# Layer 1 feed-forward: the up projection of 19 of its 22 tiles as seven block products

## The chip, the cores and the metric

The kernel runs on one core of a Trainium2 chip. The metric is the device time of one execution in microseconds; the median of three runs is given. The engines that matter are TensorE (matmuls, shown as PE, with its weight loads as PEld), VectorE (DVE), ScalarE (ACT), GpSimd (POOL) and the queue of DMA starts on SyncE (SP).

## The reference, cut to what matters

Two layers run over 640 token columns: 512 of a denoising sample and 128 of a prompt, side by side. Each layer is a mixer followed by a convolutional feed-forward. The change concerns the feed-forward of layer 1:

```python
def _conv_ffn(h, w_up, cw, cb, w_down):      # h: tokens x 1024, w_up: 1024 x 5632, w_down: 2816 x 1024
    a, g = jnp.split(h @ w_up, 2, axis=-1)   # a and g: tokens x 2816 each
    return (jax.nn.gelu(_dwconv3(a, cw, cb)) * g) @ w_down
...
h = _modulate(x, norm2_w[l], sh2, sc2)       # RMS norm, scale and shift
x = x + g2 * _conv_ffn(h, ...)
```

## The kernel before, in words

Everything is feature-major: a tile is 128 features (partitions) by 640 tokens (columns), and the columns are worked on as two halves of 320 (`HF`). The model width 1024 is 8 tiles (`KT`), the inner width 2816 is 22 tiles (`NF`).

Matmuls run on float32 split in two parts of type fp32r: hi is the rounded value, lo what is left of it. `wload` (L177) loads a weight tile of 128 x 1024, ScalarE casts it to hi (L181), and VectorE subtracts to get lo (L183); raw, hi and lo tiles have rings of three buffers each (`wraw`, `whi`, `wlo`). `proj` (L186, its matmul is L193) multiplies hi by hi, hi by lo and lo by hi, for each of the 8 k tiles and each half: 8 x 3 x 2 = 48 matmuls of 320 columns for one output tile of 640 columns.

`ffn` (L323) runs over the 22 tiles f. For each it makes two output tiles with `up` (L324), one of a and one of g: 96 matmuls. `hidden` (L333) copies a out of PSUM (L310), runs the three-tap convolution (ScalarE L313, four VectorE instructions L317 and L319, because the sample and the prompt are separate sequences), gelu (L336), the product with g (L337), and splits the result to hi and lo (L197, L198). The down projection goes by groups of 8, 7 and 7 tiles (`GROUPS`, L27). After the first tile of the next group, `down` (L342) makes all eight output tiles of the group before, and `residual` (L268, L273) adds each to x in three instructions (columns 0 to 320, 320 to 512, 512 to 640, since the gate of the prompt differs). The last group goes through `out_halves` (L276), which takes the halves one after the other, so that the norm of the first half can be made beside the matmuls of the second; it also squares the new x (L214) and sums on GpSimd (L215).

At its start `start_three` (L293) begins three up tiles on the first half while the norm of the second half is still being made (`norm_k`, L244).

PSUM has eight banks: three tiles of two banks for products (tag A twice, tag B once, L72) and two banks for all else (`misc`).

The order of instructions on each engine is fixed when the program is built: the tile framework takes instructions by priority (program order, moved by `tc.high_priority`) as their inputs and buffers become free in its own model of the engines. It can therefore put matmuls of a later step between those of an earlier one.

Of the kernel before, what the change touches and what calls it, by code (L numbers as in the profile page):

```python
# [8 lines left out]
F32 = mybir.dt.float32  # L9
# [36 lines left out]
def trunk(ctx: ExitStack, tc: tile.TileContext, I, O):  # L46
# [130 lines left out]
    def wload(src, n, key="w"):  # L177
        raw = wp.tile([P, 1024], F32, tag="wraw", name=nm("wraw"), bufs=3)
        nc.sync.dma_start(out=raw[:, :n], in_=src)
        hi = wp.tile([P, 1024], F32R, tag="whi", name=nm("whi"), bufs=3)  # L180
        S.copy(hi[:, :n], raw[:, :n])  # L181
        lo = wp.tile([P, 1024], F32R, tag="wlo", name=nm("wlo"), bufs=3)
        V.tensor_tensor(out=lo[:, :n], in0=raw[:, :n], in1=hi[:, :n], op=ALU.subtract)  # L183
        return hi, lo

    def proj(ps, hi, lo, hs, off=0, halves=(0, 1), ks=None):  # L186
        n = len(hs) if ks is None else KT
        for k in (range(n) if ks is None else ks):
# [54 lines left out]

    def norm_k(pool, xk, rb, l, js, jc, k, hl, a0, a1):  # L244
# [3 lines left out]
        hf = pool.tile([P, w], F32, tag="hf", name=nm("hf"), bufs=2)  # L248
# [5 lines left out]
        S.copy(hl[:, 0, a0:a1], hf)  # L254
        eng = G if k % 2 else V
        eng.tensor_tensor(out=hl[:, 1, a0:a1], in0=hf, in1=hl[:, 0, a0:a1], op=ALU.subtract)

# [18 lines left out]
    def out_halves(pool, x, src, n, l, j, ys, acc, xsrc, done):  # L276
        late = []
        for b in range(2):
            for o in range(KT):
                hi, lo = wload(src(o), n * P)  # L280
# [12 lines left out]
    def start_three(srcs, hs, late):  # L293
        tiles = []
        for i, src in enumerate(srcs):
            hi, lo = wload(src, KT * P)
# [11 lines left out]
    def conv3(pool, ps, w0, w1, w2, b, tag, bufs=2):  # L308
        a = pool.tile([P, NT], F32, tag=tag + "a", name=nm(tag + "a"), bufs=bufs)
        S.copy(h2(a), ps[:, :, :HF])  # L310
        t = pool.tile([P, NT], F32, tag=tag + "t", name=nm(tag + "t"), bufs=bufs)
# [10 lines left out]

    def ffn(pool, x, hs, l, acc, between, done, late):  # L323
        def up(f, s):  # L324
            for _ in range(1 + (f %3 == 1)):
                if between:
                    between.pop(0)()
            hi, lo = wload(I["w_up"][l, f, s], KT * P)
            ps = mm_tile()
            proj(ps, hi, lo, hs)  # L330
            return ps

        def hidden(f, pa, pg):  # L333
            w = [vc_("fcw", (l * 3 + i) * NF + f) for i in range(3)]
            _, t = conv3(pool, pa, w[0], w[1], w[2], vc_("fcb", l * NF + f), "fc")
            S.activation(out=t, in_=t, func=AF.Gelu_apprx_tanh)  # L336
            mark[0] = V.tensor_tensor(out=h2(t), in0=h2(t), in1=pg[:, :, :HF], op=ALU.mult)  # L337
            hl = hl_tile(hidp, "hid") if f % 10 < 9 else hl_tile(pool, "hidx", 1)
            hilo(hl, t)
            return hl  # L340

        def down(g, hid):  # L342
            f0, f1 = GROUPS[g]
            for o in range(KT):
                if between:
                    between.pop(0)()
                hi, lo = wload(I[f"w_down{g}"][l, o], (f1 - f0) * P)
                ps = mm_tile()
                proj(ps, hi, lo, hid)
                residual(x[o], ps, l, 5, o, 0, NT)  # L350

        first = start_three([I["w_up"][l, 0, 0], I["w_up"][l, 0, 1], I["w_up"][l, 1, 0]], hs, late)
        pend = None
        for g, (f0, f1) in enumerate(GROUPS):
            hid = []
            for f in range(f0, f1):
                pa = first.pop(0) if first else up(f, 0)
                pg = first.pop(0) if first else up(f, 1)
                hid.append(hidden(f, pa, pg))
                if pend is not None:  # L360
                    down(*pend)
                    pend = None
            pend = (g, hid)
        return out_halves(pool, x, lambda o: I["w_down2"][l, o], 7, l, 5, pend[1], acc, None, done)

    def mixer0(ctx0, pool, hs, ready):
# [18 lines left out]
        def token_major(name, evict, before=None):  # L385
            pss = [mm_tile() for _ in range(3)]
            for kk in range(KT // 2):
                if before is not None and kk == 0:
                    before(-1)
                hi, lo = wload(I[name][kk], 1024)  # L390
                for k2 in range(2):
# [47 lines left out]
        def gmlp(g):  # L439
            hi, lo = wload(I["w_gu"][g], KT * P)  # L440
            ps = mm_tile("B")
# [30 lines left out]
        def q_part(h):  # L472
            hi, lo = wload(I["w_qk"][0, h], KT * P)
            ps = mm_tile("B" if h else None)
            proj(ps, hi, lo, hs)
            raw = ap_.tile([P, NT], F32, tag="qraw", name=nm("qraw"), bufs=1)
            with tc.high_priority(300):
                S.activation(out=h2(raw), in_=ps[:, :, :HF], func=AF.Copy, scale=0.125)
            q = ap_.tile([P, NT], F32, tag="q", name=nm("q"), bufs=1)
            rope(q[:, :NS], raw[:, :NS])  # L480
            S.copy(q[:, NS:], raw[:, NS:])
            return q

# [120 lines left out]
    def mixer1(ctx1, gpool, hs, firsts):  # L604
# [98 lines left out]
        def head_in(h, hook=None):  # L703
            xcs, xch, xmh = [], [], []
            for i in range(2):
# [23 lines left out]
        def head_v(h, xmh):  # L729
            hi, lo = wload(I["w_hv"][h], 512)  # L730
            va = pool.tile([P, NCH, HD + 1], F32, tag="va", name=nm("va"), bufs=1)
# [14 lines left out]
        def head_qk(h, xch):  # L746
            hi, lo = wload(I["w_hqk"][h], 1024)
            qk = []
# [98 lines left out]
        def head_og(h, part=(0, 1)):  # L847
            sgs = []
            for o in (2 * h + i for i in part):
                hi, lo = wload(I["w_og"][o], KT * P)  # L850
                ps = mm_tile()
# [109 lines left out]
    with ExitStack() as c0:  # L961
# [17 lines left out]

        late = ffn(xp, x, hs, 0, acc, btw, done0, late)  # L980
        modx.close()
# [4 lines left out]
    with ExitStack() as c0:  # L986
        xp, x, acc = xpool(c0)
        hs = []
        late = out_halves(xp, x, lambda o: I["w_out1"][o], KT, 1, 2, ys, acc, xdr,
                   lambda b: norm_half(xp, x, acc, 1, 3, 4, hs, b))  # L990

        def done1(b):
# [7 lines left out]

            return rstd_steps(xp, acc, b, rb) + [lambda k=k: one(k) for k in range(KT)]

        for step in ffn(xp, x, hs, 1, acc, [], done1, late):
            step()
# [5 lines left out]
def _layout(i):  # L1010
# [67 lines left out]
    dn = np.asarray(i["w_down"])  # L1078
    for g, (f0, f1) in enumerate(GROUPS):
        a[f"w_down{g}"] = np.stack([wt(dn[l, f0 * P:f1 * P]) for l in range(2)])  # L1080
    t = np.arange(NS)
# [40 lines left out]
```

## Time and profile before

| | |
|---|---|
| median of three runs | 1606.1 us (1604.69 to 1607.99) |
| profiled execution, its own time | 1606.81 us |
| its span, first to last instruction | 1605.0 us |
| TensorE busy | 1561.2 us, 10560 matmuls |
| VectorE busy | 960.0 us |
| ScalarE busy | 712.7 us |
| GpSimd busy | 120.1 us |
| granted TensorE clock, mean | 0.992 |

Busy time is the union of an engine's instructions, so overlapping matmuls are not counted twice; a single matmul's duration is much longer than the distance at which matmuls follow one another. Layer 1's feed-forward runs from about 1100 us (its norm and its first up tiles) to the end. Idle time in brackets stands before an instruction, with the instruction that ended it.

### The profile page before, as it was taken

The page shows a single profiled execution, that of the slowest core. Times are in us where ns is not written, and L with a number is a line of the kernel's source. Part 1 is how long each engine was busy: PE and PEld are TensorE (multiplying, and loading weights), DVE is VectorE, ACT ScalarE, POOL GpSimd, SP SyncE. Part 2 cuts the span into 40 slices and gives each one's busy share as a digit, 9 for nine tenths or more (in the row PEclk, how much of TensorE's full clock was granted, in tenths as well). Part 3 has the DMA queues.
Part 4 walks back from the last instruction along what each step waited for, and adds up shares of the span by engine and source line. Part 5 has one row for each costly group of instructions (what it writes and reads, how often), then busy time and mean ns, then how long its engine had stood idle before and what let it go on. Part 6 is the DMA issues. An engine that isn't in the chain of part 4 may idle for free.

```text
span 1605.0 us, 26031 instructions
## 1 busy us (share of the span) xinstructions
PE 1561.2 (97%) x10560; PEld 1501.9 (94%) x10560; DVE 960.0 (60%) x1738; ACT 712.7 (44%) x1171; POOL 120.1 (7%) x116
## 2 busy tenths in 40 slices
PE   5999999999999999999989999999999999999997
PEld 4888889999999999999988999999999999999996
DVE  5547776769894889444775575667544334433445
ACT  5646665563312331334587564635633223312342
POOL 1100002300000000002300000013100000000012
PEclk9999999999999999999998999999999999999998
DMA  9424444436562555224523213234322222222233
GB/s 359 149 73 146 150 146 172 134 101 201 170 208 89 176 176 175 83 62 123 165 69 95 85 57 90 66 135 128 93 79 79 67 79 79 65 81 79 72 107 112
DMA packets 60167, 191.60 MB, mean 119 GB/s; under 512 B 6764, under 2 KB 10348, under 8 KB 59920
## 3 DMA queue, kind: packets, MB, share of 16 engines
q1 hardware_dynamic: 60048, 189.95, 37.2%
q8 instruction: 83, 1.36, 0.4%
q14 instruction: 36, 0.29, 0.1%
HBM read 181.95 MB, written 7.97 MB: 118 GB/s over the span
## 4 chain that ended last, share of the span: by engine, by line
PE 86%; DVE 6%; ACT 4%; issue 2%; DMA 2%; POOL 0%; SPq 0%; POOLq 0%; DVEq 0%; ACTq 0%
PE mm L193 72%; PE mm L827 2%; PE mm L805 2%; DVE wlo L183 1%; PE mm L401 1%; PE mm L403 1%; PE mm L802 1%; PE mm L402 1%; DMA mw<-w_mod 1%; PE misc L562 1%; ACT whi L181 1%; DVE xr L247 1%; ACT hf L252 1%; PE misc L109 1%; PE mm L532 1%
## 5 line engine op out<-in xcount | busy, mean ns | idle before, releaser
L193 PE MATMUL mm<-h,whi 128*128 128x320 f32 x3744 | 726.7, 312 | 3.4 <-ACT rows L612 1.6
L193 PEld LDWEIGHTS mm<-h,whi 128*128 128x128 f32 x3744 | 595.4, 189 | 9.7 <-ACT fca L310 1.9
L181 ACT CAST whi<-wraw 128x1024 fp32r<-128x1024 f32 (+2 forms) x229 | 233.0, 1019 | 586.6 <-PE mm L193 551.5
L193 PE MATMUL mm<-h,wlo 128*128 128x320 f32 x1872 | 444.8, 311 | 3.4 <-DVE wlo L183 3.4
L183 DVE TENSOR_TENSOR wlo<-wraw,whi 128x1024 fp32r<-128x1024 f32 (+2 forms) x229 | 272.7, 1191 | 232.8 <-ACT whi L181 226.3
L193 PE MATMUL mm<-hid,whi 128*128 128x320 f32 x1920 | 393.1, 310 | 1.8 <-ACT hid L197 0.7
L193 PEld LDWEIGHTS mm<-h,wlo 128*128 128x128 f32 x1872 | 318.9, 189 | 5.3 <-DVE wlo L183 4.2
L193 PEld LDWEIGHTS mm<-hid,whi 128*128 128x128 f32 x1920 | 310.4, 188 | 4.7 <-ACT hid L197 1.4
L193 PE MATMUL mm<-hid,wlo 128*128 128x320 f32 x960 | 255.5, 309 | 0.2 <-DVE wlo L183 0.2
L193 PEld LDWEIGHTS mm<-hid,wlo 128*128 128x128 f32 x960 | 169.7, 188 | 0.4 <-DVE wlo L183 0.4
L273 DVE SCALAR_TENSOR_TENSOR x<-mm,mod,x 128x192 f32<-128x192 f32 (+2 forms) x192 | 75.3, 433 | 139.9 <-PE mm L193 135.6
L136 DVE SCALAR_TENSOR_TENSOR mj<-mw,crow 128x1024 f32<-128x1024 f32 x112 | 136.6, 1219 | 1.0
L215 POOL TENSOR_TENSOR acc<-acc,sq 128x320 f32<-128x320 f32 x48 | 61.7, 1284 | 910.0 <-ACT sq L214 880.1
L337 DVE TENSOR_TENSOR fct<-fct,mm 128x640 f32<-128x640 f32 x44 | 36.1, 820 | 97.5 <-PE mm L193 94.1
L336 ACT ACTIVATE fct<-fct 128x640 f32<-128x640 f32 x44 | 32.3, 738 | 84.5 <-DVE fct L319 84.5
L252 ACT ACTIVATE hf<-xr,mod 128x192 f32<-128x192 f32 (+2 forms) x88 | 47.5, 575 | 22.6 <-DVE mod L174 8.8
L247 DVE TENSOR_TENSOR xr<-x,rb 128x320 f32<-128x320 f32 (+1 forms) x56 | 38.0, 694 | 24.9 <-ACT hf L252 13.7
L317 DVE SCALAR_TENSOR_TENSOR fct<-fca,vec,fct 128x511 f32<-128x511 f32 x88 | 44.9, 547 | 11.9 <-ACT fct L313 11.9
L319 DVE SCALAR_TENSOR_TENSOR fct<-fca,vec,fct 128x511 f32<-128x511 f32 x88 | 44.7, 544 | 0.0
L313 ACT ACTIVATE fct<-fca,vec 128x640 f32<-128x640 f32 x44 | 40.5, 925 | 1.3
L214 ACT ACTIVATE sq<-x 128x320 f32<-128x320 f32 x70 | 32.2, 468 | 16.7 <-DVE x L273 15.0
L541 ACT ACTIVATE p<-mm,mx 128x640 f32<-128x640 f32 (+1 forms) x40 | 28.4, 711 | 17.8 <-DVE mx L540 17.6
(249 smaller groups left out, 1491.6 us busy)
## 6 DMA issues: line engine op xcount, KB each, us to landing
wraw<-w_up SPq DMA_DIRECT2D x88, 512.0 KB, 3.7
mw<-w_modT SPq DMA_DIRECT2D x56, 512.0 KB, 4.3
wraw<-w_down SPq DMA_DIRECT2D x48, 448.0 KB, 3.3
mw<-w_mod SPq DMA_DIRECT2D x40, 512.0 KB, 5.9
wraw<-w_out SPq DMA_DIRECT2D x32, 512.0 KB, 3.6
wraw<-w_down SPq DMA_DIRECT2D x16, 512.0 KB, 3.6
x<-xT SPq DMA_DIRECT2D x16, 320.0 KB, 5.5
wraw<-w_qk SPq DMA_DIRECT2D x8, 512.0 KB, 3.5
```

The source lines that it names most:

```text
L136: V.scalar_tensor_tensor(out=junk, in0=w, scalar=1.0, in1=crow[:, r], op0=ALU.mult, op1=ALU.mult, accum_out=mod[:, l, j, k, r:r + 1])
L181: S.copy(hi[:, :n], raw[:, :n])
L183: V.tensor_tensor(out=lo[:, :n], in0=raw[:, :n], in1=hi[:, :n], op=ALU.subtract)
L193: T.matmul(ps[:, b, :HF], w, hs[k][:, part, b * HF:b * HF + HF], start=(k == 0 and i == 0), stop=(k == n - 1 and i == 2))
L215: (eng or V).tensor_tensor(out=acc[:, sl], in0=acc[:, sl], in1=sq, op=ALU.add)
L247: V.tensor_tensor(out=xr, in0=xk[:, a0:a1], in1=rb, op=ALU.mult)
L252: S.activation(out=hf[:, a:b], in_=xr[:, a:b], func=AF.Identity, scale=mod[:, l, jc, k, r:r + 1], bias=mod[:, l, js, k, r:r + 1])
L273: V.scalar_tensor_tensor(out=xo[:, a:b], in0=pa, scalar=mod[:, l, j, o, r:r + 1], in1=xo[:, a:b], op0=ALU.mult, op1=ALU.add)
L313: S.activation(out=t, in_=a, func=AF.Identity, scale=w1, bias=b)
L317: V.scalar_tensor_tensor(out=t[:, s + 1:e], in0=a[:, s:e - 1], scalar=w0, in1=t[:, s + 1:e], op0=ALU.mult, op1=ALU.add)
L319: V.scalar_tensor_tensor(out=t[:, s:e - 1], in0=a[:, s + 1:e], scalar=w2, in1=t[:, s:e - 1], op0=ALU.mult, op1=ALU.add)
L337: mark[0] = V.tensor_tensor(out=h2(t), in0=h2(t), in1=pg[:, :, :HF], op=ALU.mult)
```

## The change

Only layer 1's feed-forward is changed in its work; `wload` returns the raw tile too, layer 0 keeps its path. The first three tiles (`PLAIN`) are made as before. For the tiles 3 to 21 the two products a and g, each in two column halves, are seen as a 2 x 2 block product: the two rows are a and g, the inner index is the first and the second four k tiles, the columns are the two halves. They are made by seven block products of 4 k tiles x 3 passes = 12 matmuls of 320 columns, which need sums of weight blocks and sums of input blocks, and some of which are added to a bank that was read out before.

- Inputs: `fold_step`, four times, makes four combined input blocks (two subtractions, two combined instructions, two splits of 640 columns on VectorE, with two casts on ScalarE). They run among the three plain tiles.
- Weights: `weights(f)` loads four quarters of 256 KB, makes four sums of 512 columns on VectorE, and splits 1024 + 1024 + 1024 + 512 columns; the first two pairs use the rings `whi` and `wlo` that the down weights use as well. It is called one tile ahead.
- Banks: `fold_first`, `fold_main` and `fold_last` run the seven products into two banks of one PSUM tile and one `misc` bank. From f = 5 on that third bank begins with a ScalarE copy of the first product.
- Down: groups of 5, 5, 4, 4 and 4 tiles in layer 1; at most four (after a group of five) or three output tiles are made after each up tile. The last group, four tiles, goes through `out_halves`.
- The pool of layer 1's norm is closed after the plain tiles, and the fold's weight buffers take its place.

```diff
+GROUPS = (((0, 8), (8, 15), (15, 22)), ((0, 5), (5, 10), (10, 14), (14, 18), (18, 22)))
+PLAIN = 3
...
+        def prod(out, w, i, rhs, start):
+            for j in range(4):
+                c = slice(i * 512 + j * P, i * 512 + j * P + P)
+                for n, (h, part) in enumerate(((0, 0), (0, 1), (1, 0))):
+                    T.matmul(out, w[h][:, c], rhs(j, part), start=(start and j == 0 and n == 0),
+                             stop=(j == 3 and n == 2), skip_group_check=not start)
+
+        def split(w, src, n):
+            S.copy(w[0][:, :n], src[:, :n])
+            V.tensor_tensor(out=w[1][:, :n], in0=src[:, :n], in1=w[0][:, :n], op=ALU.subtract)
+            return w
+
+        def weights(f):
+            def pair(pool_, tag, n, bufs):
+                return [pool_.tile([P, n], F32R, tag=tag + p, name=nm(tag), bufs=bufs) for p in ("hi", "lo")]
+
+            ra, rb = (wp.tile([P, 1024], F32, tag="wraw", name=nm("wraw"), bufs=3) for _ in range(2))
+            rc = zp[0].tile([P, 1024], F32, tag="rc", name=nm("rc"), bufs=1)
+            rd = zp[0].tile([P, 512], F32, tag="rd", name=nm("rd"), bufs=2)
...
+            nc.sync.dma_start(out=rd, in_=src[1][:, hi_])
+            nc.sync.dma_start(out=ra[:, lo_], in_=src[0][:, lo_])
+            nc.sync.dma_start(out=rc[:, hi_], in_=src[1][:, lo_])
+            nc.sync.dma_start(out=rb[:, lo_], in_=src[0][:, hi_])
+            V.tensor_tensor(out=ra[:, hi_], in0=rc[:, hi_], in1=rd, op=ALU.add)
+            wa = split(pair(wp, "w", 1024, 3), ra, 1024)
+            V.tensor_tensor(out=rb[:, hi_], in0=ra[:, hi_], in1=ra[:, lo_], op=ALU.add)
+            wb = split(pair(wp, "w", 1024, 3), rb, 1024)
+            V.tensor_tensor(out=rc[:, hi_], in0=rc[:, hi_], in1=ra[:, lo_], op=ALU.add)
+            V.tensor_tensor(out=rc[:, lo_], in0=rb[:, lo_], in1=rb[:, hi_], op=ALU.add)
+            wc = split(pair(zp[0], "zc", 1024, 2), rc, 1024)
+            wd = split(pair(zp[0], "zd", 512, 2), rd, 512)
+            return wa, wb, wc, wd
+
+        def fold_first(f, w):
+            px = mm_tile("A")
+            b1 = px[:, 0, :HF]
+            prod(b1, w[0], 0, lambda j, p: part_of(hs[j], p, 0), True)
+            return px
+
+        def fold_main(f, w, px):
+            b1, b4, b2 = px[:, 0, :HF], px[:, 1, :HF], aux[f % 2][:, :HF]
+            seed = f > PLAIN + 1
...
+            prod(b4, w[0], 1, lambda j, p: fold[j](0, p), True)
+            with tc.high_priority(200):
+                S.copy(b2 if seed else a[:, lo_], b1)
+                S.copy(g, b4)
+            prod(b2, w[1], 0, lambda j, p: part_of(hs[j + 4], p, 0), not seed)
+            prod(b1, w[1], 1, lambda j, p: fold[j](1, p), False)
+            with tc.high_priority(200):
+                S.copy(a[:, hi_], b1)
+                if seed:
+                    S.copy(a[:, lo_], b2)
+                else:
+                    V.tensor_tensor(out=a[:, lo_], in0=b2, in1=a[:, lo_], op=ALU.add)
+            prod(b4, w[2], 0, lambda j, p: part_of(hs[j + 4], p, 1), False)
+            with tc.high_priority(200):
+                V.tensor_tensor(out=a[:, hi_], in0=b4, in1=a[:, hi_], op=ALU.add)
+            prod(b1, w[2], 1, lambda j, p: fold[j](2, p), False)
+            with tc.high_priority(200):
+                V.tensor_tensor(out=g, in0=b1, in1=g, op=ALU.add)
+            return conv(f, None, a), g
+
+        def fold_last(f, w, px, t, g):
+            b1 = px[:, 0, :HF]
+            prod(b1, w[3], 0, lambda j, p: fold[j](3, p), False)
+            for sl, q in ((slice(0, HF), b1), (slice(HF, NT), g)):
+                V.scalar_tensor_tensor(out=t[:, sl], in0=t[:, sl], scalar=-1.0, in1=q, op0=ALU.mult, op1=ALU.mult)
+            return store(f, t)
...
+        for f in range(PLAIN, NF):
+            g = group_of[f]
+            px = fold_first(f, w)
+            if open_ is not None:
+                hids.append(fold_last(*open_))
+            if f > PLAIN and group_of[f - 1] != g:
+                f0, f1 = groups[g - 1]
+                todo = [(g - 1, hids[f0:f1], o) for o in range(KT)]
+            nxt = weights(f + 1) if f + 1 < NF else None
+            t, gg = fold_main(f, w, px)
+            n = min(len(todo), 4 if g and groups[g - 1][1] - groups[g - 1][0] == 5 else 3)
+            for i in range(n):
+                down(*todo.pop(0), "AB"[(n - i) % 2])
+            open_ = (f, w, px, t, gg)
+            w = nxt
```

## Rows read from the trace of the kernel before

**Rows 1.** The page's busy times: engine, busy us (share of span), instructions.

```profile
PE 1561.2 (97%) x10560; PEld 1501.9 (94%) x10560; DVE 960.0 (60%) x1738; ACT 712.7 (44%) x1171; POOL 120.1 (7%) x116
```

**Rows 2.** Chain that ended last, 1085 to 1605: start us, us, what.

```profile
1146.90 425.52 PE mm L193 x2898
1576.70 12.34 PE mm L193 x84
```

**Rows 3.** Stretches: busy us (instructions) by engine, clock, DMA share, GB/s.

```profile
400.00:600.00 200.00, 200.00 (x1366) 200.00 (x1365) 156.37 (x257) 60.23 (x70) 0.00 (x0) 1.00 0.54 166
1160.00:1500.00 340.00, 340.00 (x2321) 340.00 (x2320) 132.70 (x198) 101.73 (x117) 0.00 (x0) 1.00 0.25 76
```

**Rows 4.** Instruction groups, 1085 to 1605: busy us, mean ns, idle before.

```profile
L183 DVE TENSOR_TENSOR wlo<-wraw,whi 128x1024 fp32r<-128x1024 f32 x60 | 73.7, 1228 | 96.9 <-ACT whi L181 96.9
L181 ACT CAST whi<-wraw 128x1024 fp32r<-128x1024 f32 x60 | 62.8, 1049 | 196.6 <-PE mm L193 191.7 <-issue 4.9
L317 DVE SCALAR_TENSOR_TENSOR fct<-fca,vec,fct 128x511 f32<-128x511 f32 x22 | 16.5, 751 | 7.6 <-ACT fct L313 7.6
L317 DVE SCALAR_TENSOR_TENSOR fct<-fca,vec,fct 128x127 f32<-128x127 f32 x22 | 7.6, 345 | 0.0
L198 DVE TENSOR_TENSOR hid<-fct,hid 128x640 fp32r<-128x640 f32 x20 | 16.4, 819 | 0.0
L197 ACT CAST hid<-fct 128x640 fp32r<-128x640 f32 x20 | 14.6, 729 | 3.6 <-DVE fct L337 3.5
L273 DVE SCALAR_TENSOR_TENSOR x<-mm,mod,x 128x320 f32<-128x320 f32 x27 | 14.9, 550 | 81.9 <-PE mm L193 81.9
L273 DVE SCALAR_TENSOR_TENSOR x<-mm,mod,x 128x192 f32<-128x192 f32 x32 | 13.1, 410 | 11.0 <-PE mm L193 10.9
L273 DVE SCALAR_TENSOR_TENSOR x<-mm,mod,x 128x128 f32<-128x128 f32 x32 | 10.9, 341 | 0.0
L240 ACT COPY rb<-misc 128x320 f32<-128x320 f32 x2 | 0.8, 424 | 6.2 <-PE misc L236 6.2
```

**Rows 5.** Instruction groups of the whole span: the split of 512 columns.

```profile
L183 DVE TENSOR_TENSOR wlo<-wraw,whi 128x512 fp32r<-128x512 f32 x4 | 2.8, 688 | 10.2 <-ACT whi L181 10.2
```

**Rows 6.** VectorE in order of time: start us, us, engine, instruction.

```profile
1211.45 1.22 DVE L183 TENSOR_TENSOR wlo<-wraw,whi 128x1024 fp32r<-128x1024 f32 x1
1212.59 0.82 DVE L198 TENSOR_TENSOR hid<-fct,hid 128x640 fp32r<-128x640 f32 x1
```

**Rows 7.** TensorE in order of time, within one product of out_halves.

```profile
1103.51 0.70 PE L236 MATMUL misc<-dg,ones 128*128 128x320 f32 x2
1103.80 0.70 PE L193 MATMUL mm<-hid,whi 128*128 128x320 f32 x2
```

**Rows 8.** Waits, 1085 to 1605: us in total, times, longest us.

```profile
ACT whi L181 <- PE mm L193: 253.9, 73, 6.0
```

**Rows 9.** Stretches where layer 1's up projection starts.

```profile
1120.00:1125.00 5.00, 4.26 (x30) 4.00 (x29) 3.84 (x6) 3.49 (x5) 2.68 (x3) 1.00 0.23 49
1145.00:1150.00 5.00, 4.29 (x29) 3.96 (x28) 2.93 (x5) 4.79 (x7) 0.00 (x0) 1.00 0.29 70
```

**Rows 10.** Stretches of layer 1's mixer around a TensorE wait.

```profile
840.00:850.00 10.00, 8.06 (x29) 6.39 (x28) 3.82 (x8) 4.98 (x13) 0.00 (x0) 0.62 0.41 81
850.00:860.00 10.00, 10.00 (x57) 9.80 (x57) 2.88 (x5) 7.25 (x16) 1.51 (x2) 0.70 0.50 137
```

**Rows 11.** TensorE in order of time: that wait, in brackets.

```profile
842.75 0.90 PE L193 MATMUL mm<-h,wlo 128*128 128x320 f32 x2 [1.94 <-DVE wlo L183]
```

**Rows 12.** VectorE in out_halves: the same split twice.

```profile
1578.62 1.08 DVE L183 TENSOR_TENSOR wlo<-wraw,whi 128x896 fp32r<-128x896 f32 x1
1581.32 1.70 DVE L183 TENSOR_TENSOR wlo<-wraw,whi 128x896 fp32r<-128x896 f32 x1
```

**Rows 13.** GpSimd in order of time, beside the second split.

```profile
1581.20 0.88 POOL L215 TENSOR_TENSOR acc<-acc,sq 128x320 f32<-128x320 f32 x1 [2.73 <-ACT sq L214]
```

**Rows 14.** DMA starts, 1085 to 1605: count, KB each, us to landing.

```profile
wraw<-w_up SPq DMA_DIRECT2D x44, 512.0 KB, 3.6
```

More of the change, by code (lines that the diff above doesn't have):

```diff
@@ L321, in conv3, with ffn @@
         return a, t
-    def ffn(pool, x, hs, l, acc, between, done, late):
+    def ffn(pool, x, hs, l, between, late, fold=None, enter=None):
+        abufs = 2 if fold is None else 1
+        groups = GROUPS[l]
+        zc = ExitStack()
+        zp = [None]
         def up(f, s):
-            for _ in range(1 + (f %3 == 1)):
+            for _ in range(1 + (f % 3 == 1)):
                 if between:
                     between.pop(0)()
-            hi, lo = wload(I["w_up"][l, f, s], KT * P)
+            hi, lo, _ = wload(I["w_up"][l, f, s], KT * P)
             ps = mm_tile()
@@ L339, in hidden, with store @@
+        def store(f, t):
+            hl = hl_tile(hidp, "hid") if fold is not None or f % 10 < 9 else hl_tile(pool, "hidx", 1)
             hilo(hl, t)
             return hl
[L342 to L350, printed above, removed]
@@ L352, in ffn @@
-        first = start_three([I["w_up"][l, 0, 0], I["w_up"][l, 0, 1], I["w_up"][l, 1, 0]], hs, late)
[L353 to L363, printed above, removed]
@@ L364, in ffn, with hidden, down @@
-        return out_halves(pool, x, lambda o: I["w_down2"][l, o], 7, l, 5, pend[1], acc, None, done)
+        def hidden(f):
+            pa = first.pop(0) if first else up(f, 0)
+            pg = first.pop(0) if first else up(f, 1)
+            t = conv(f, pa)
+            mark[0] = V.tensor_tensor(out=h2(t), in0=h2(t), in1=pg[:, :, :HF], op=ALU.mult)
+            return store(f, t)
+        def down(g, hid, o, tag=None):
+            f0, f1 = groups[g]
+            if between:
+                between.pop(0)()
+            hi, lo, _ = wload(I[f"w_down{l}_{g}"][o], (f1 - f0) * P)
+            ps = mm_tile(tag)
+            proj(ps, hi, lo, hid)
+            residual(x[o], ps, l, 5, o, 0, NT)
@@ new lines, in fold_last @@
+        def fold_last(f, w, px, t, g):
[3 more added lines that the diff above has]
+                V.scalar_tensor_tensor(out=t[:, sl], in0=t[:, sl], scalar=-1.0, in1=q, op0=ALU.mult, op1=ALU.mult)
+            return store(f, t)
+        first = start_three([I["w_up"][l, 0, 0], I["w_up"][l, 0, 1], I["w_up"][l, 1, 0]], hs, late)
+        first = list(first)
+        if fold is None:
+            pend = None
+            for g, (f0, f1) in enumerate(groups):
+                hid = []
+                for f in range(f0, f1):
+                    hid.append(hidden(f))
+                    if pend is not None:
+                        for o in range(KT):
+                            down(*pend, o)
+                        pend = None
+                pend = (g, hid)
+            return pend[1]
@@ new lines, in ffn @@
+        hids = [hidden(f) for f in range(PLAIN)]
+        enter()
+        zp[0] = zc.enter_context(tc.tile_pool(name="zp", bufs=1))
+        aux = [ms_tile() for _ in range(2)]
+        group_of = {f: g for g, (f0, f1) in enumerate(groups) for f in range(f0, f1)}
+        w = weights(PLAIN)
+        open_, todo = None, []
+        for f in range(PLAIN, NF):
[13 more added lines that the diff above has]
+            w = nxt
@@ L986, in trunk @@
     with ExitStack() as c0:
[L987 to L990, printed above, removed]
+        xp = c0.enter_context(tc.tile_pool(name="xp1", bufs=1))
+        x = [xp.tile([P, NT], F32, name=nm("x"), tag=f"x{k}") for k in range(KT)]
+        tt = [xp.tile([P, 2, NT], F32R, name=nm("tt"), tag=f"tt{k}") for k in range(4)]
+        sc = ExitStack()
+        sp = sc.enter_context(tc.tile_pool(name="sp", bufs=1))
@@ new lines, in trunk, with fold_step @@
+        late = out_halves(sp, x, lambda o: I["w_out1"][o], KT, 1, 2, ys, acc, xdr, half)
+        tt += [hl_tile(hp, "h") for _ in range(2)]
+        btw = []
+        def fold_step(j):
+            if j == 0:
+                tt.extend([hl_tile(hidp, "hid") for _ in range(2)])
+            d = hidp.tile([P, 4, HF], F32, tag="hid", name=nm("fd"), bufs=9)
+            b11, b12, b21, b22 = f0[j], f1[0][:, j], f0[j + 4], f1[1][:, j]
+            V.tensor_tensor(out=d[:, 0], in0=b11, in1=b12, op=ALU.subtract)
+            V.tensor_tensor(out=d[:, 2], in0=b22, in1=b12, op=ALU.subtract)
+            V.scalar_tensor_tensor(out=d[:, 1], in0=d[:, 0], scalar=-1.0, in1=b22, op0=ALU.mult, op1=ALU.subtract)
+            V.scalar_tensor_tensor(out=d[:, 3], in0=d[:, 1], scalar=-1.0, in1=b21, op0=ALU.mult, op1=ALU.subtract)
+            for i in range(2):
+                hilo(tt[2 * j + i], d[:, 2 * i:2 * i + 2].rearrange("p i c -> p (i c)"))
@@ L992, in done1 @@
+        fold = [lambda i, p, j=j: tt[2 * j + i // 2][:, p, (i % 2) * HF:][:, :HF] for j in range(4)]
+        hid = ffn(xp, x, hs, 1, [lambda j=j: fold_step(j) for j in range(4)], late, fold, sc.close)
+        ep = c0.enter_context(tc.tile_pool(name="ep", bufs=1))
+        acc = ep.tile([P, NT], F32, name=nm("acc"), tag="acc")
         def done1(b):
@@ L999, in one @@
                 nc.sync.dma_start(out=O["yT"][k][:, sl], in_=x[k][:, sl])
-            return rstd_steps(xp, acc, b, rb) + [lambda k=k: one(k) for k in range(KT)]
-        for step in ffn(xp, x, hs, 1, acc, [], done1, late):
+            return rstd_steps(ep, acc, b, rb) + [lambda k=k: one(k) for k in range(KT)]
+        for step in out_halves(ep, x, lambda o: I["w_down1_4"][o], 4, 1, 5, hid, acc, None, done1):
             step()
```

87 lines of the change are left out of this document (60 added, 27 removed).

## The prediction

> **What bounds the kernel now.** I read the page's busy times first: TensorE is busy for 1561.2 of 1605.0 us [rows 1], the others far less. Then the chain of waits: from 1146.90 on, 2898 matmuls stand in it for 425.52 us without a break, 146.8 ns each [rows 2], so in layer 1's feed-forward a matmul that is taken out shortens the chain by 146.8 ns, until something else is late. In the table of stretches 1160 to 1500 has 340.00 of 340 us TensorE, 132.70 VectorE, 101.73 ScalarE [rows 3]: much room beside. Last, durations by shape [rows 4, 5], and who waits: ScalarE's weight cast stands 253.9 us behind TensorE [rows 8], because its ring of three tiles is full; today that costs nothing.
>
> **Removed.** A plain tile has 96 matmuls of 320 columns, a folded one 7 x 12 = 84. 19 folded tiles save 19 x 12 = 228; 228 x 146.8 ns = 33.5 us. The new products run 12 matmuls in a row into one bank, where the old ones alternate two. `out_halves` does that already: 84 matmuls in 12.34 us, 146.9 ns [rows 2]. So the pace stays. Down matmuls are as many as before.
>
> **VectorE in a folded tile.** Four sums of 512 columns at 0.688 (the split of that width, also two inputs [rows 5]), 2.75; splits 3 x 1.228 + 0.688 = 4.37; convolution twice 0.751 + 0.345, 2.19 (L319 taken as L317); two bank sums of 320 columns at about 0.5, 1.0, the two last products at 0.550, 1.1, and the hid split 0.82 [rows 4]. Sum 12.2 us in 17 instructions. Back to back they follow 0.08 us sooner than their durations say (1.22 long, the next 1.14 later [rows 6]), so 10.9 us. TensorE needs 84 x 0.1468 = 12.3 us. VectorE is then 89% full in the nine tiles without a down product (3, 4, 7 to 9, 12, 13, 17, 21). Layer 0's stretch 400 to 600 has 156.37 of 200 us VectorE beside an unbroken TensorE [rows 3]; 89% no row shows. Bounds: 0, and 9 x 1.3 = 12 us if VectorE can be filled to 90% only and no overlap is left (12.2 / 0.9 = 13.6). I take 2, since the weights come one tile ahead and the tiles with downs have slack: there four downs add 4 x (0.82 + 0.55 + 0.41 + 0.34) = 8.5 us VectorE to 17.6 us TensorE.
>
> **ScalarE**: casts 3 x 1.049 + under 0.729, four copies at 0.424, activations and the hid cast as before [rows 4]; about 8 of 12.3 us, hidden. A copy has one product (1.76 us) or more before its bank is wanted; behind a 1.049 cast it ends 1.5 us after, just in time. Nothing, or what the no-down term holds.
>
> **Down products in twos to fours.** 16 have 30 matmuls, 16 have 24. Their weights use the ring of three pairs, in which two pairs now belong to the next folded tile. So a second down tile can be cast only when the first is done: 22 of the 32 downs stand behind another one. If TensorE takes nothing in between, each costs cast 0.729 + split 0.819 = 1.55 us (640 columns [rows 4]), 34 us in all. At best 0: the order is laid out by readiness, down to single matmuls; a broadcast of the norm (L236) stands in the middle of a product of `out_halves` [rows 7]. What can fill in: the last product of the open tile and the first two of the next, 3 x 1.76 us, as many as there are gaps between four downs. I take 4 us (0.2 each), near the filled end, because such an order needs only that the model's cast is not much shorter than the chip's.
>
> **The fold's start.** The fold's buffers take the memory of the norm pool, whose inputs the third tile's g product reads through its first four k tiles, until 24 x 0.1468 = 3.5 us before its end. Two of its four loads wait for that, and SP's later ones stand behind them: landing 3.6 [rows 14], sum 0.69, cast 1.05 make 5.3, a gap of 1.8 us. And VectorE is late: four fold steps of 4 x 0.55 + 2 x 0.82 = 3.8, 15 us, beside three tiles of 3.8 and three splits of 1.23, 15 us, where TensorE gives 21 us and the idle VectorE time before. Between 0 and 8 us; I take 3. What the clock adds: waits under a microsecond left it at 1.00 [rows 9]; a stretch with a wait of 1.94 [rows 11] ran at 0.62 and the next at 0.70 [rows 10], 3.8 + 3.0 = 6.8 us of full clock. A gap of 3 us may or may not bring it down: I take 3 of 6.8. Together 6.
>
> **The tail.** Each of `out_halves`' 16 steps falls from 21 to 12 matmuls, 1.76 us (the rest has moved into the groups before). In the second half VectorE has split 0.69, residual 0.41 + 0.34, one final product 0.55: 2.0, or 1.7 back to back; just full. A GpSimd sum beside a split makes it 1.70 instead of 1.08 [rows 12, 13]. Raw buffers: (3.6 + 0.7 + 0.7) / 3 = 1.7 us a step, just enough. From 0 to 16 x 0.62 = 10 us; I take 3. The chain after the last matmul stays, as does the norm before (same instructions, other tiles).
>
> **Sum.** 33.5 - 2 - 4 - 6 - 3 = 18.5 us. 1606.8 (profiled execution: span 1605.0 and 1.8 around it) - 18.5 = 1588.3; the median of the runs is 0.7 lower, so 1588.
>
> **Rivals.**
> - Nearly all is hidden: 33.5 less 0 to 6, 1573 to 1579. For it: the unbroken TensorE beside VectorE at 78% [rows 3]. Against: the fold's start has no cover. 0.13.
> - VectorE becomes the bound: 12 us in the no-down tiles, 8 at the start with the clock unharmed, 4 downs, 4 tail: 28 of 33.5 lost, 1600. For it: 12.2 isolated against 12.3. Against: the 0.08 us overlap. 0.17.
> - Slower: the ring of three pairs. If the down products stay in a row on TensorE, 22 x 1.55 = 34 us, with the other terms 11: 33.5 - 45 = -11.6, 1618. It decides from 22.5 / 22 = 1.0 us a gap. For it: the cast waits behind TensorE even now [rows 8]; against: filling [rows 7]. [...] 0.10.
> - Slower by the clock. In 840 to 860 waits at bank and weight hand-overs went with a mean of 0.66 [rows 10, 11]. The folded tiles with their downs hold 19 x 84 + 864 = 2460 matmuls, 361 us; six such 20 us stretches at 6.8 make 41 us lost, less the 33.5: 1614. Against: short waits left the clock at 1.00 [rows 9]. 0.03. [...]
> - No change: several of these add up to the gain, 1603 to 1609. 0.05.
>
> **How the numbers follow.** The forecast's own case, 1580 to 1595, has 0.52. Faster: 0.52 + 0.13 + 0.17 = 0.82; same (0.2% is 3.2 us, about what a measurement can tell) 0.05; slower 0.13. From 1574 to 1604 all but both slower cases, half of no change and the lowest edge are held, about 0.82.
>
> **What would show it.** Right: 10332 matmuls; 146.8 ns a matmul in folded tiles; TensorE idle mostly in one gap of some 3 us where the first folded tile begins, VectorE near 90% busy between downs. The ring rival shows as ScalarE's cast ending TensorE waits of 1 us or more between down tiles; the VectorE rival as waits for weight splits or bank sums in tiles 7 to 9 and 12, 13; the clock rival in the granted clock. Wrong would be a pace above 150 ns without waits, or waits spread over every tile.

## The result, and the profile after

| | before | after |
|---|---|---|
| median of the runs | 1605.6 us (1604.7 to 1608.0) | 1628.6 us (1626.2 to 1634.1) |
| span of the profiled execution | 1605.0 us | 1627.4 us |

The ratio is 1.0145, with a 95% interval from 1.0117 to 1.0174: slower by some 23 us, where 18 us faster was forecast. The time lies outside the range.

The page's busy times after, which answer to [rows 1]:

```profile
PE 1545.9 (95%) x10332; PEld 1468.1 (90%) x10332; DVE 1090.9 (67%) x1999; ACT 761.1 (47%) x1288; POOL 119.0 (7%) x116
```

The 228 matmuls are gone (10560 to 10332). Up to 1085 us the two traces agree within 1.3 us. The stretches after it, which answer to [rows 3, 9, 10] (span, then busy us and count of PE, PEld, DVE, ACT, POOL, then clock, DMA share, GB/s):

```profile
1160.00:1175.00 15.00, 7.67 (x53) 7.41 (x51) 13.94 (x27) 8.10 (x12) 0.00 (x0) 0.92 0.16 54
1175.00:1200.00 25.00, 23.46 (x143) 22.39 (x144) 21.64 (x32) 12.85 (x19) 0.00 (x0) 0.91 0.31 96
1200.00:1540.00 340.00, 318.03 (x2074) 303.97 (x2073) 228.07 (x384) 134.62 (x200) 0.00 (x0) 1.00 0.25 74
```

and the last of them in the kernel before:

```profile
1200.00:1540.00 340.00, 340.00 (x2321) 340.00 (x2320) 131.73 (x197) 100.44 (x116) 0.00 (x0) 1.00 0.25 75
```

Read the count, not only the busy time. From 1200 to 1540 the kernel before has 2321 matmuls in an unbroken row, this one 2074: 247 fewer, and 247 x 146.7 ns = 36.2 us. The busy column gives up only 22.0 us, because a matmul lasts 309 to 323 ns in this trace (means by group) while the next one starts 146.7 ns after it, so the last one's end lies over the first 0.16 us of each wait. The weight loads (PEld), 188 ns each, give up 36.0. The clock is 1.00, so all of this is waiting.

So I counted the loss another way, called "by the distances" from here on: from 1146 to the last matmul of the last group, the distance from the start of each matmul to the start of the next, less 146.7 ns. Before it is 0.2 us, after 57.0. New waits of 56.7 against the 33.5 saved make +23.2; the spans differ by 22.4. Of the 57.0, 11.6 lie where the fold starts (1167 to 1200), 41.0 in the folded tiles and their down products (1200 to 1583), 4.2 in the last group.

Who ends TensorE's waits, 1160 to 1600 (us in total, times, longest; L376 is the matmul of `prod`, L197 that of `proj`):

```profile
PE misc L376 <- ACT misc L421: 10.7, 9, 1.3
PE mm L376 <- ACT w L380: 7.8, 1, 7.8
PE mm L197 <- ACT whi L182: 7.6, 14, 0.7
PE mm L197 <- DVE wlo L184: 2.3, 4, 0.6
PE mm L376 <- DVE fcg L436: 2.0, 3, 1.0
PE mm L376 <- DVE w L381: 1.9, 3, 0.8
PE mm L376 <- ACT fca L426: 1.5, 3, 0.7
```

The largest is a bank copy: L421, the copy of the first product into the `misc` bank, before the third product (the seed copy). By the distances it costs 12.2 us. Second are the down products' weight casts (L182) and splits (L184): 9.1 and 3.0 us by the distances in the folded tiles. Third is the one gap at the start. Waits that VectorE ended in the folded tiles come to 5.0, copies into `fca` to 0.9. The other 10.9 of the 41.0 us are delays below 0.3 us: the matmul after each of these waits comes 0.10 us late too, and many hand-overs are too short to show as idle time.

**One copy, from close by.** TensorE around a first fold product that follows the downs (start us, us, in brackets the idle time before it):

```profile
1239.46 0.46 PE L197 MATMUL mm<-hid,wlo 128*128 128x320 f32 x2
1239.76 0.31 PE L376 MATMUL mm<-h,w 128*128 128x320 f32 x1
1239.90 1.04 PE L376 MATMUL mm<-tt,w 128*128 128x320 f32 x6
...
1241.22 0.60 PE L376 MATMUL mm<-hid,w 128*128 128x320 f32 x3
1243.14 2.02 PE L376 MATMUL misc<-h,w 128*128 128x320 f32 x12 [1.32 <-ACT misc L421]
```

ScalarE in the same microseconds:

```profile
1239.66 1.05 ACT L380 CAST w<-wraw 128x1024 fp32r<-128x1024 f32 x1 [4.91 <-PE mm L197]
1241.72 1.04 ACT L380 CAST w<-wraw 128x1024 fp32r<-128x1024 f32 x1 [1.00 <-PE mm L376]
1242.67 0.42 ACT L421 COPY misc<-mm 128x320 f32<-128x320 f32 x1
```

The first product (its last matmul is the row at 1239.76) had ended by 1240.1, ScalarE was idle from 1240.71 to 1241.72, and still its copy ran at 1242.67 only. Two things hold it. It stands behind the cast of the next tile's second pair, which waits until this tile's first pair is used up, since the ring holds three pairs. In this trace the copy starts 0.95 us after that cast has started (1241.72 to 1242.67), 0.09 us before its end.

But the copy is late where no cast stands ahead of it, too. In an early folded tile, the end of the first product, the second one and the third:

```profile
1178.73 0.87 PE L376 MATMUL mm<-h,w 128*128 128x320 f32 x3
1179.43 1.04 PE L376 MATMUL mm<-tt,w 128*128 128x320 f32 x6
...
1180.75 0.60 PE L376 MATMUL mm<-hid,w 128*128 128x320 f32 x3
1181.19 1.92 PE L376 MATMUL misc<-h,w 128*128 128x320 f32 x12
1182.95 1.04 PE L376 MATMUL mm<-tt,w 128*128 128x320 f32 x6
```

and the copy:

```profile
1181.39 0.43 ACT L421 COPY fca<-mm 128x320 f32<-128x320 f32 x1 [0.58 <-PE mm L376]
```

ScalarE stood idle, and what ended its idle time is the second product's last matmul (the three from 1180.75), not the first product's, which had started before 1179.43. The two products have different banks, but both banks belong to one tile (`px`), and in this program the waits go by tile, as e5 and e9 show below: the copy out of one bank starts at 1181.39, 0.04 us after the product in the other is complete (1181.35). The third product, the one seeded by that copy, is next on TensorE: nothing covers it. (In this tile, not yet seeded, the third product needs no copy: it follows without a gap, 12 matmuls in 1.76 us.)

**The start.** TensorE, then VectorE, the queue of DMA starts (SPq) and ScalarE:

```profile
1167.22 0.46 PE L197 MATMUL mm<-h,wlo 128*128 128x320 f32 x2
1175.44 0.90 PE L376 MATMUL mm<-h,w 128*128 128x320 f32 x2 [7.76 <-ACT w L380]
1176.70 2.90 PE L376 MATMUL mm<-h,w 128*128 128x320 f32 x10 [0.36 <-DVE w L381]
...
1168.83 0.48 DVE L1150 SCALAR_TENSOR_TENSOR fd<-fd,f 128x320 f32<-128x320 f32 x1
...
1169.40 0.33 SPq L393 DMA_DIRECT2D rd<-w_up  x1
...
1173.48 0.68 DVE L397 TENSOR_TENSOR wraw<-rc,rd 128x512 f32<-128x512 f32 x1
...
1174.35 1.04 ACT L380 CAST w<-wraw 128x1024 fp32r<-128x1024 f32 x1
```

One gap, as forecast, but 7.8 us and not 3. The fold steps read the memory of the norm pool, which the fold's weight buffers take over. The last read (L1150) ends at 1169.31, 1.6 us after the last plain matmul, and the fold's first load starts right behind it, at 1169.40. Load, sum and cast then take the 6.0 us to the first fold product. Then ten matmuls take 2.73 us, 273 ns each, most of them at a granted clock of 0.50:

```profile
1173.00:1179.00 6.00, 3.20 (x11) 2.80 (x11) 6.00 (x8) 3.73 (x5) 0.00 (x0) 0.50 0.15 53
```

From 1180 to 1200 the granted clock is 1.00 again.

### The profile page after: what moved, and what is told of

It is laid out like the page before. It is cut to its first block, busy times and chain, and to the rows that moved or that the text cites. A ratio compares the mean times of both kernels' runs of the same rounds, so it can differ in the third digit from the quotient of the medians.

```text
span 1627.4 us, 26120 instructions
## 1 busy us (share of the span) xinstructions
PE 1545.9 (95%) x10332; PEld 1468.1 (90%) x10332; DVE 1090.9 (67%) x1999; ACT 761.1 (47%) x1288; POOL 119.0 (7%) x116
## 5 line engine op out<-in xcount | busy, mean ns | idle before, releaser
L197 PE MATMUL mm<-h,whi 128*128 128x320 f32 x2480 | 490.8, 313 | 3.3 <-ACT rows L732 1.6
L197 PE MATMUL mm<-hid,whi 128*128 128x320 f32 x1984 | 409.1, 312 | 10.2 <-ACT whi L182 7.6
L197 PEld LDWEIGHTS mm<-h,whi 128*128 128x128 f32 x2480 | 396.7, 189 | 9.0 <-ACT fca L317 1.9
L182 ACT CAST whi<-wraw 128x1024 fp32r<-128x1024 f32 (+3 forms) x207 | 193.6, 937 | 388.9 <-PE mm L197 342.7
L197 PEld LDWEIGHTS mm<-hid,whi 128*128 128x128 f32 x1984 | 319.3, 188 | 20.2 <-ACT whi L182 14.2
L184 DVE TENSOR_TENSOR wlo<-wraw,whi 128x1024 fp32r<-128x1024 f32 (+3 forms) x207 | 227.2, 1099 | 155.4 <-ACT whi L182 154.4
L197 PE MATMUL mm<-h,wlo 128*128 128x320 f32 x1240 | 299.9, 312 | 2.7 <-DVE wlo L184 2.7
L197 PE MATMUL mm<-hid,wlo 128*128 128x320 f32 x992 | 260.7, 310 | 4.9 <-DVE wlo L184 4.9
L197 PEld LDWEIGHTS mm<-h,wlo 128*128 128x128 f32 x1240 | 212.7, 190 | 4.3 <-DVE wlo L184 3.2
L197 PEld LDWEIGHTS mm<-hid,wlo 128*128 128x128 f32 x992 | 174.2, 188 | 6.8 <-DVE wlo L184 6.7
L376 PE MATMUL mm<-h,w 128*128 128x320 f32 x342 | 66.8, 316 | 9.9 <-ACT w L380 7.8
L376 PEld LDWEIGHTS mm<-h,w 128*128 128x128 f32 x342 | 54.9, 192 | 11.6 <-ACT w L380 8.0
L381 DVE TENSOR_TENSOR w<-wraw,w 128x1024 fp32r<-128x1024 f32 x38 | 46.3, 1219 | 11.9 <-ACT w L380 11.9
L251 DVE TENSOR_TENSOR xr<-x,rb 128x320 f32<-128x320 f32 (+1 forms) x56 | 37.4, 683 | 24.6 <-ACT hf L257 11.1
L376 PE MATMUL mm<-h,zc 128*128 128x320 f32 x285 | 48.9, 312 | 1.5 <-ACT fca L426 1.5
```

What stands on the lines that cost most here:

```text
L197: T.matmul(ps[:, b, :HF], w, part_of(hs[k], part, b), start=(k == 0 and i == 0), stop=(k == n - 1 and i == 2))
L376: T.matmul(out, w[h][:, c], rhs(j, part), start=(start and j == 0 and n == 0), stop=(j == 3 and n == 2), skip_group_check=not start)
L381: V.tensor_tensor(out=w[1][:, :n], in0=src[:, :n], in1=w[0][:, :n], op=ALU.subtract)
```

## The experiments

All edits are to the changed kernel. Times beside the kernel before on the same chip:

| run | median us | ratio to before | TensorE waits that changed |
|---|---|---|---|
| changed kernel | 1628.6 | 1.0145 [1.0117, 1.0174] | |
| e1 second pair, own ring | 1625.4 | 1.0125 [1.0100, 1.0151] | whi 1.0, but fca 10.6 |
| e2 down pair, own ring | 1600.2 | 0.9969 [0.9953, 0.9985] | seed copy 0.8, whi 0.6 |
| e3 no seed copy | 1613.2 | 1.0053 [1.0037, 1.0068] | seed copy 0, whi 2.4 |
| e4 four plain tiles | 1627.8 | 1.0140 [1.0112, 1.0169] | start 2.5 |
| e5 own tile for each bank | 1594.9 | 0.9934 [0.9917, 0.9950] | seed copy 0.7, whi 2.4 |
| e6 = e5 + e2 | 1587.0 | 0.9880 [0.9864, 0.9896] | start alone left |
| e7 = e6 + fold on GpSimd | 1588.8 | 0.9894 [0.9872, 0.9916] | start 6.0, but 1.9 before it |
| e8 = e6 + sums on GpSimd | 1607.0 | 1.0016 [0.9998, 1.0034] | fca 7.7, start 8.7 |
| e9 copy before second product | 1626.1 | 1.0139 [1.0112, 1.0165] | wait moved |
| e10 = e5 + e1 | 1593.8 | 0.9932 [0.9909, 0.9955] | seed copy 0, whi 0.6 |
| e11 one third pair | 1631.3 | 1.0171 [1.0145, 1.0197] | |
| e12 = e6 + four plain tiles | 1582.8 | 0.9874 [0.9846, 0.9902] | start 3.7 |

The first theory was the ring of three pairs (the rival of the prediction), against VectorE and the start. **e1** and **e2** give one user of the ring a ring of its own:

```diff
# e1 (and zc, zd, rd with one buffer, for the memory)
-            wb = split(pair(wp, "w", 1024, 3), rb, 1024)
+            wb = split(pair(zp[0], "zb", 1024, 2), rb, 1024)
# e2, in down() of the fold (and zc with one buffer)
-            hi, lo, _ = wload(I[f"w_down{l}_{g}"][o], (f1 - f0) * P)
...
+                hi, lo = split([zp[0].tile([P, 640], F32R, tag="d" + p, name=nm("d" + p), bufs=2) for p in ("hi", "lo")], raw, n)
```

> The fold's second weight pair leaves the ring of three that it shares with the first pair and the down weights, and gets two buffers of its own; to make room, the third and fourth pair and the raw quarter have one buffer instead of two. Ring theory (the loss is TensorE waiting for casts and bank copies that stand on ScalarE behind a cast with no free buffer): in the changed kernel 12.2 us of matmul waits end with the seed copy and 14.4 us with a down cast or split, so 1628.5 falls by 20 to 27 us, to 1602 to 1609, and the waits of the seed copy vanish from TensorE's list. VectorE theory (the folded tile simply needs 12.2 us of VectorE beside 12.3 us of TensorE): 1625 to 1632, as the VectorE work is the same.

> Only the down weights leave the shared ring, for two buffers of their own (the third pair has one buffer instead of two for the room). Ring theory: the 14.4 us behind down casts and splits go, the seed copy's 12.2 us stay since the second pair's cast still waits for the first pair's buffer ahead of the copy: 1612 to 1616. VectorE theory: 1625 to 1632.

e1 missed. The waits for down weights did go, but the copies' waits grew. The waits of e1:

```profile
PE misc L376 <- ACT misc L421: 10.8, 16, 1.2
PE mm L376 <- ACT fca L426: 10.6, 15, 1.1
```

Almost every folded tile now waits for a copy, twice, with no ring to blame: there is a second cause. TensorE's order shows why it grew: from 1200 to 1540 fold products and down products (L376 and L197) take turns 42 times in e1 and 123 times in the changed kernel, so less stands between a product and the copy that it needs. e2 did better than its theory, which had 1612 to 1616. In its trace (lines from L376 on stand 6 later) TensorE has down matmuls where the copy would be waited for:

```profile
1302.94 0.60 PE L382 MATMUL mm<-hid,w 128*128 128x320 f32 x3
1303.60 0.85 PE L197 MATMUL mm<-hid,dhi 128*128 128x320 f32 x4
1304.28 1.92 PE L382 MATMUL misc<-h,w 128*128 128x320 f32 x12
```

Its last row is the third product; the four down matmuls stand between the second and it, and it waits for nothing. **e11** makes the memory concession of e2 alone, and gains nothing:

```diff
-            wc = split(pair(zp[0], "zc", 1024, 2), rc, 1024)
+            wc = split(pair(zp[0], "zc", 1024, 1), rc, 1024)
```

> The changed kernel with one buffer instead of two for the third pair and nothing else, the side condition of e2, e6 and e7. If that buffer matters neither way: 1624 to 1632. If part of e2's 28 us came from it: under 1620.

**e3** takes the seed copy away (the third product starts its bank, and VectorE adds afterwards); **e4** gives the fold's inputs one more plain tile of time:

```diff
-            seed = f > PLAIN + 1
+            seed = False
-PLAIN = 3
+PLAIN = 4
```

> The third bank is never seeded by a copy; its product starts the bank and VectorE adds the first product's copy afterwards, as the changed kernel does in tiles 3 and 4 (17 more sums of 320 columns, 0.49 us each, on VectorE). Ring theory: the product no longer waits for the ScalarE copy; 12.2 us of TensorE waits go, up to 3 come back at the next product into the copied bank: 1616 to 1620. VectorE theory: 17 x 0.49 = 8 us more of VectorE work, 1630 to 1637.

> Four plain tiles instead of three: 12 more matmuls, 1.8 us. Start theory (the fold's buffers wait for the fold steps, which VectorE finishes 2 us after the last plain matmul, and 11.6 us are lost there): the fold steps end within the fourth plain tile, the gap shrinks to loading, sum and cast after the last plain inputs, 2 to 4 us, so 1628.5 - 8 + 1.8 = 1621 to 1624. Rival (VectorE's debt only moves on): the wait shows up in the first folded tiles instead, 1628 to 1631.

e3 is 15 us below the changed kernel, more than the ring theory allowed, and VectorE's 17 more bank sums did not hurt: the seed copy, which was costed at nothing, is a main cause. e4 cut the start's wait from 7.8 to 2.5 us and pays 1.8 for 12 more matmuls. Its profiled execution is 3.8 us shorter (span 1623.6 against 1627.4), but the medians don't tell the two apart, so its gain is not shown.

**e5** tests the wait by whole tiles: the three banks become three tiles (and one more folded tile is seeded).

```diff
-            b1, b4, b2 = px[:, 0, :HF], px[:, 1, :HF], aux[f % 2][:, :HF]
-            seed = f > PLAIN + 1
+            b1, b4, b2 = px[:, 0, :HF], aux[0][:, :HF], aux[1][:, :HF]
+            seed = f > PLAIN
```

> The fold's second product gets a tile (bank) of its own in misc instead of the second bank of the first product's tile, and the third product the other misc tile in every folded tile. Whole-tile theory: in the changed kernel the copies out of the first bank wait for the second product (they are released by its last matmul, though it writes the other bank), so a copy stands bare between second and third product: 12.2 us before the third product, 2 us and the short gaps before the fifth. With own tiles they have a product of 1.76 us as cover: 1628.5 falls by 12 to 17 us, to 1611 to 1617; waits for down casts stay at about 14 us. Ring theory alone: the copy stays behind the second pair's cast, which is released only by the second product, so the wait before the third product stays: 1624 to 1630.

33.7 us below the changed kernel, as much as all that the fold saves, and twice what its theory asked for: the waits for down casts, which were to stay, fell from 7.6 to 2.4 us as well. Why they did was not tried. **e9** turns the theory round: banks as in the changed kernel, the copy ahead of the second product.

```diff
+            with tc.high_priority(200):
+                S.copy(b2 if seed else a[:, lo_], b1)
             prod(b4, w[0], 1, lambda j, p: fold[j](0, p), True)
             with tc.high_priority(200):
-                S.copy(b2 if seed else a[:, lo_], b1)
                 S.copy(g, b4)
```

> The changed kernel with one statement moved: the copy out of the first product's bank stands before the second product in program order. Whole-tile theory: the copy now waits for the first product alone, but the second product, which writes the other bank of the same tile, waits for the copy; so the bare copy of 0.7 us moves from the third to the second product, in all 19 folded tiles where nothing fills it: TensorE waits move to the second product, and the time stays within 10 us of 1628.5. Bank theory (only the same bank is waited for): the second product runs beside the copy and the waits vanish, 1610 to 1616 as with own tiles but the fifth product.

The waits of e9 (the copy is L420 here):

```profile
PE mm L197 <- ACT whi L182: 9.6, 16, 1.4
PE mm L376 <- ACT misc L420: 6.6, 7, 1.0
```

and one of the seven, the first matmuls of a second product:

```profile
1239.45 1.14 PE L376 MATMUL mm<-tt,w 128*128 128x320 f32 x6 [1.02 <-ACT misc L420]
```

The wait for the copy moved from the third product (`misc`) to the second (`mm`), which neither reads nor writes the bank that is copied; the time is the same. In this program a bank copy and a product of one tile did not run beside each other in either order: waits of up to 1.3 us in the changed kernel, of up to 1.0 here.

**e6** has both, own tiles and the own ring of e2; **e10** has own tiles and the ring of e1.

> Both: own tiles for the products and two own buffers for the down weights. Both theories together: the down ring alone measured 1600.2 and still had a few us of copy waits; 1592 to 1598. If the down ring had taken all of it: 1599 to 1602.

> e1 (second weight pair with buffers of its own, 1625.4 us, no gain, against the ring theory) with the own tiles of e5. If e1 failed because its bare copies took what its ring gave (27 us of waits for copies in its trace), own tiles set the gain free: 1584 to 1590, as e6. If e1 failed because its third and fourth pair had one buffer: 1598 or more.

e6 came out 5 us below its expected range, e10 between its two cases. e6 from 1200 to 1540, and all its TensorE waits from 1150 on (lines numbered as in e2):

```profile
1200.00:1540.00 340.00, 340.00 (x2319) 339.88 (x2318) 248.41 (x423) 148.99 (x222) 0.00 (x0) 1.00 0.26 81
```

```profile
PE mm L382 <- ACT w L386: 7.8, 1, 7.8
PE misc L240 <- DVE dg L236: 2.4, 2, 1.8
PE misc L228 <- DVE acc L219: 1.9, 1, 1.9
PE mm L197 <- DVE wlo L184: 0.8, 1, 0.8
PE mm L197 <- ACT whi L182: 0.6, 1, 0.6
```

TensorE has no break again, 2319 matmuls against 2321 before, and beyond the start there are left the two waits of the final norm (L228, L240), which the kernel before has too, and two under a microsecond. The copy has the cover that the prediction counted on; a tile's first product, the last product of the tile before, the second and the third product, then ScalarE:

```profile
1261.08 1.92 PE L382 MATMUL mm<-h,w 128*128 128x320 f32 x12
1262.84 1.04 PE L382 MATMUL mm<-tt,zd 128*128 128x320 f32 x6
...
1264.60 1.04 PE L382 MATMUL misc<-tt,w 128*128 128x320 f32 x6
...
1266.36 1.92 PE L382 MATMUL misc<-h,w 128*128 128x320 f32 x12
...
1263.03 0.41 ACT L427 COPY misc<-mm 128x320 f32<-128x320 f32 x1 [10.13 <-PE mm L382]
```

The copy is released by the first product and is done 3 us before the third product starts. Alone, own tiles bring 33.7 us and the down ring 28.4 (e2's runs spread from 1595 to 1604); together 41.6, so about 20 us can be had by either: a covered copy, or something else to do while it is waited for. The loss by the distances in the folded tiles says the same: 41.0 us in the changed kernel, 11.1 in e2, 10.6 in e5, 0.1 in e6. e10 is as fast as e5: with own tiles, e1's ring gives nothing measurable.

**e7** and **e8** move VectorE work of e6 to GpSimd: two of the subtractions in `fold_step`, or the four weight sums.

```diff
# e7, and the same for d[:, 2]
-V.tensor_tensor(out=d[:, 0], in0=b11, in1=b12, op=ALU.subtract)
+G.tensor_tensor(out=d[:, 0], in0=b11, in1=b12, op=ALU.subtract)
# e8, and the same for the other three sums
-V.tensor_tensor(out=ra[:, hi_], in0=rc[:, hi_], in1=rd, op=ALU.add)
+G.tensor_tensor(out=ra[:, hi_], in0=rc[:, hi_], in1=rd, op=ALU.add)
```

> As before, and two of the four input combinations of each fold step are made by GpSimd (8 x 0.49 us off VectorE). Start theory: the fold's first weights wait for VectorE's fold steps, 8 us of TensorE idle and 1.3 us at the lower clock; 4 us less VectorE work shortens the gap by 3 to 4 us: 3 to 5 us faster than without. Rival: GpSimd's own 0.9 us per instruction and its slowing of VectorE eat it: same within 2 us.

> As e6, and the four weight sums of each folded tile are made by GpSimd instead of VectorE: 2.75 of 12.2 us a tile off VectorE. VectorE theory: the tiles without downs get faster, 5 us or more in all. Hand-over theory (TensorE waits for chains of casts and copies, not for VectorE's amount of work): within 3 us of e6, or slower, since a GpSimd sum takes twice as long or more and stands in the chain of the first pair.

e7 shortens the gap at the start (7.8 to 6.0 us) and not the time: a plain tile before it now waits 1.9 us for VectorE, which it did not in e6. e8 is 20 us slower than e6. The slowest and the fastest of its four sums, by count, busy us and mean ns, then VectorE's split of the first two pairs:

```profile
L407 POOL TENSOR_TENSOR rc<-rc,wraw 128x512 f32<-128x512 f32 x19 | 40.2, 2116 | 0.3
...
L403 POOL TENSOR_TENSOR wraw<-rc,rd 128x512 f32<-128x512 f32 x19 | 25.2, 1326 | 250.9 <-DMA rc<-w_up 194.4 <-ACT fct L348 31.0 <-issue 17.8
L387 DVE TENSOR_TENSOR w<-wraw,w 128x1024 fp32r<-128x1024 f32 x38 | 65.0, 1714 | 26.2 <-ACT w L386 25.8
```

In e6 each sum takes 0.69 us and that split 1.22: the sums take two to three times as long, and the splits beside them take 1.71, as one did beside a GpSimd sum in [rows 12, 13] (1.70 instead of 1.08).

**e12** is e6 with `PLAIN = 4`:

> e6 with four plain tiles. The start is the largest wait left in e6 (8.0 us idle and 2.6 us at the lower clock). In e4 the fourth plain tile cut it to 2.7 us idle; 1.8 us are paid for 12 more matmuls: 1587.0 - 5.3 - 2 + 1.8 = 1581 to 1583. If the debt of VectorE only moves on, as e4's total (same as the changed kernel) may mean: 1586 to 1589.

It came out as expected, 1582.8 us (1581.4 to 1588.1), and is the fastest: 21 us below the kernel before on that chip. Now that the start's gap is nearly the only one, closing it seems to count: 4 us below e6, but the runs overlap, so this is not shown.

## Why the prediction was wrong

- **The saving was right.** 228 fewer matmuls, and 146.7 ns a matmul where nothing is waited for, 12 in a row into one bank too. Without the new waits in the folded tiles the change gives what was forecast: e6 has 1587.0, against 1588 predicted. That it is so near is luck: in e6 the start costs 9.8 us where 6 were taken, and the folded tiles nothing where 6 were (2 for VectorE, 4 for the downs).
- **ScalarE is the step that failed**: "A copy has one product (1.76 us) or more before its bank is wanted [...] Nothing". I counted that cover from the end of the product that the copy reads. The copy is released one product later, since the second product is in the other bank of the same tile, and then nothing is left of it. It measured 12.2 us before the third products and 1.9 before the fifth. The nine waits before the third products were 0.74 us twice, behind the cast of the next tile's fourth pair (0.62 us), and 1.31 to 1.34 seven times, behind that of its second pair (1.05 us). For a copy with nothing ahead of it, 0.7 us is an estimate by the distances: 0.04 from the second product's end to the copy (at 1181.39), 0.42 of copy, 0.05 to the third product (at 1243.14), and the 0.16 that a wait costs beside its idle time. e5 removes the tile, e3 the copy, e9 moves the wait: all three agree.
- **Down products**: 4 us taken, 12.1 measured in the folded tiles (9.1 cast, 3.0 split), some 0.55 for each of 22 gaps, where the bounds were 0 and 34. The expectations of e1 and e2 have 14.4; the trace gives 13.8 with the last group's waits. The ring rival asked for 1.0 us a gap to make the change slower; by itself it did not. It took part in the copies' waits as well, by the cast that stood ahead of them (0.95 us in the one shown). e2 removes it. No rival had the copies by themselves.
- **The start**: 6 taken, 11.6 measured: the gap is 7.8 instead of 3, at the far end of its bounds. I let the third tile's g product release the memory of the norm pool, 3.5 us before its end, and counted VectorE's fold steps (30 us of VectorE work against 21 us of TensorE and the idle time before) as a matter of its own. But the fold steps read that memory too: the last of them releases it, 1.6 us after the last plain matmul, and load, sum and cast all come behind it. The granted clock of 0.50 cost 1.3 of it, on the ten matmuls at 273 ns instead of 146.7, where 3 were taken.
- **VectorE** at 89%: 2 us taken. The waits that VectorE ended in the folded tiles sum to about 4 as idle time, 5 by the distances, and in e6, with the same VectorE work, TensorE has none. One of e6's tiles without a down product has VectorE at 86% beside an unbroken TensorE, so that share is no bound here:

```profile
1275.16:1287.48 12.32, 12.32 (x87) 12.32 (x86) 10.63 (x18) 7.39 (x11) 0.00 (x0) 1.00 0.27 85
```

- **The tail**: 3 taken, 4.2 measured.
- **The clock rival** did not come: 1.00 from 1200 to 1540, with 31 waits of 0.2 to 1.3 us in it.
- **Not settled**: why the planner laid out fewer down matmuls between the products in e1, and why own tiles took most of the down casts' waits along in e5. The 10.9 us of delays below 0.3 us can't be divided between the two causes; e6, which removes both, has 0.1 us of loss left in the folded tiles.

By the sum: 33.5 - 2 - 4 - 6 - 3 was forecast; 33.5 less 56.7 was measured, of which in the folded tiles 13 are copies, 12 downs, 5 VectorE and 11 the short delays, and besides 12 the start and 4 the tail.

## What to carry to other kernels

When a cover is counted, look at what releases the covered instruction, not only at how long it takes: here a copy of 0.42 us left TensorE idle for up to 1.3 us, nine times, because it was released by a product that it does not read. Give each accumulating bank that is read out between products a tile of its own (33.7 us here), and give tiles that live for different times rings of their own (28.4 us for the down weights). A wait is gone as well when other ready work can be put into it, so two cures of one wait don't add up (41.6 us together).

## What the runs showed that I had not expected

- Each of the 31 waits of TensorE (0.2 to 1.3 us) from 1200 to 1540 cost 0.16 us more than the idle time that the profile shows before the next matmul, and the matmul after that came 0.10 us late; in that stretch, with many short hand-overs besides, 36 us were lost against 22 shown as idle. The count of matmuls and the weight loads' busy time show the whole.
- Four sums of 512 columns on GpSimd took 1.3 to 2.1 us instead of 0.69, and the split beside them 1.71 instead of 1.22: 52 us of sums taken off VectorE lowered its busy time by 14 us only (1090.5 to 1076.6).
- The granted clock was 0.50 from 1173 to 1179, in and after the one wait of 7.8 us; from 1200 to 1540 waits up to 1.3 us left it at 1.00.
